# Rotating the late products over eight PSUM banks, splitting the last weight blocks into passes of 192 and 128 columns, and taking GpSimd out of the final norm

## The chip, the cores and the metric

The kernel runs on one core of one Trainium2 chip. The metric is the device time of one execution in microseconds (us), as a median over runs. Before the change it is 1042.79 us over three runs (1041.4 to 1043.75).

A core has five engines that run beside each other, each through its own instructions in order: PE (TensorE, matrix products into PSUM, with its weight loads shown apart as PEld), DVE (VectorE), ACT (ScalarE), POOL (GpSimd) and SP (SyncE, which here issues every DMA). PSUM has eight banks of 512 fp32 columns.

## The reference, cut to what matters

One decoder layer on 1024 prompt tokens and 64 sample tokens, 1088 columns in all, with a model width of 1024. The late part, which the change touches, is this:

```python
y_a = (o_a.astype(h.dtype) * jax.nn.silu(z_a)) @ w_up_gla
...
y_b = (o_b.astype(h.dtype) * jax.nn.silu(z_b)) @ w_up_gdn
merged = jax.nn.sigmoid(gate_a) * y_a + jax.nn.sigmoid(gate_b) * y_b
h = h + merged @ w_out
h = h + jax.nn.sigmoid(h @ w_ple_gate) * (p @ w_ple)
...
y = rms_norm(h, final_norm_w)
```

Ahead of it stand the input norm, the product with `w_in` (4,000-odd columns of projections) and two linear-attention recurrences; the change leaves them as they are.

## The kernel before, in words

Everything is kept transposed: the 128 partitions hold channels, the columns hold tokens. A width of 1024 is thus eight row blocks (m = 0 to 7) of 128 channels. The 1088 columns are cut into three chunks c, `CH = [(0, 384), (384, 384), (768, 320)]`.

**Products.** An fp32 product is made as three products of rounded halves: `w_split` (L169) cuts a 128x1024 weight block into a high half on ACT (`wh`, L173) and a low half on DVE (`wl`, L174), both float32r, and the operands are cut in the same way. `prod` (L290) then runs, for each of k = 8 row blocks, high by high, high by low and low by high, 24 matmuls into one PSUM bank (6 where k is 2). After every sixth matmul but the last it lets a list of side tasks advance by one tick (`sd.tick`); a side task is a generator that yields how many ticks it wants to wait.

**PSUM.** Two pools share the eight banks: `mp` has 3 banks (tile function `mps`, L145), `rp` has 5 (`rps`, L142). In the first two thirds of the program the 5 belong to the recurrences. In the late part every large product takes a bank of `mp`, and only the column sums of the final norm take one of `rp`.

**The late part (L1240 to L1430).** It has four stages: two branches (`py`, L1274, into M), the output product (`ho`, L1323, into H = residual + product), and the embedding stage with the final norm (L1383 to L1430). In the embedding stage, for a row block m and a chunk c, PE makes the gate product `eg` from Hh and Hl (24 matmuls) and the embedding product `ep` from ph and pl (6 matmuls). Then: ACT takes the tanh of `eg` into `et` (L1344); DVE computes (et + 1) * ep (L1420) and adds half of it to H (L1421); ACT squares H into `es` (L1425); DVE adds that to the running sum `acc` of the chunk (L1426); ACT scales H by the final norm's weight (L1428). Chunks 0 and 1 go together through m = 0 to 7; then chunk 2 goes through m = 0 to 7 with the eight weight blocks loaded and split a second time.

**The final norm of chunks 0 and 1** is a side task (`final`, L1349): a matmul with a matrix of ones sums `acc` over the partitions (`ssy`, L1354), then `normed` (L1358) takes Ln and Exp on ACT to get the reciprocal root `rsy` (L1367, L1368; these need another activation table than tanh, so there is a table load on either side), then eight products of H with `rsy` per chunk give `y` (L1379, and L1377 for the last one, which takes in the weight). Those for row blocks 2 and 5 are on POOL, the others on DVE. Each pair of row blocks leaves with one DMA (L1381).

**The end.** For m = 7 of chunk 2 the `ep` product goes first, ACT halves it (L1401), and after the `eg` product the chunk is cut into two halves of 160 columns. For each half: tanh, three DVE steps (L1407, L1410, L1411), a matmul of the squares with ones on top of the sums of the rows before (L1404, L1412), Ln, Exp, eight products (POOL takes rows 2 and 5), and DMAs of 2 + 2 + 4 row blocks for the first half, 4 + 4 for the second.

The order on each engine is set by the framework's scheduler from the program text, with a few fixed pairs (`after`). The weight pools hold three split blocks (`wh`, `wl`, 3 buffers each), so three of them can be kept at once.

Of the kernel before, what the change touches and what calls it, by code (L numbers as in the profile page):

```python
# [17 lines left out]
P = 128  # L18
# [4 lines left out]
EPS = 1e-6  # L23
NBLK = 34
NWARM = 4
SK = 2
UW, HW = 1116, 544
ORDER = ("h7 h3 g0 g2 h1 g1 k0 q0 a2 g3 h4 q1 k1 v0 a1 h5 q2 a0 "
# [75 lines left out]
def tile_hybrid_step(ctx: ExitStack, tc: tile.TileContext, xT, pT, wmain, wv0, wv1, wup, wout, wpg, wpl, wgate,  # L104
# [16 lines left out]
    def unit(name, dt=F32):  # L121
        return up.tile([P, UW], dt, tag="u", name=name)
# [13 lines left out]
    def wide(name):  # L136
        return up.tile([P, 384], F32, tag="wide", name=name, bufs=4)
# [44 lines left out]
    def w_next():  # L182
        if not wready:
            w_split()
        r = wready.pop(0)
        return r
# [115 lines left out]
    def xprod(ps, c, ws, hh, ll, lo_last=False):  # L302
        prod(ps, CH[c][1], ws, 0, lambda k: hh[c][:, k], lambda k: ll[c][:, k], 8, lo_last=lo_last)
# [944 lines left out]
    w_load()  # L1248
    w_load()


    M = [None] * 8

    def branch(br, og, first, after=None):
        for m in range(8):
            spilled = f"{'gh'[br]}{m}" in gscr
            while len(wready) < 2 - spilled:
                w_split()
            ws = None if spilled else w_next()
            us = w_next()  # L1260
            if first:
                M[m] = unit(f"M{m}") if m < 6 else lp.tile([P, UW], F32, tag="M", name=f"M{m}", bufs=2)
            for c, (o, w) in enumerate(CH):
                if spilled:
                    t = lp.tile([P, 384], F32, tag="gt", name=f"gt{br}{m}{c}", bufs=3)
                    load(t[:, :w], gscr[f"{'gh'[br]}{m}"][:, o:o + w])
                else:
                    pg = mps(f"pg{br}{m}{c}")
# [5 lines left out]
                py = mps(f"py{br}{m}{c}")  # L1274
# [39 lines left out]
    for m in range(8):  # L1314
        xres.append(unit(f"xres{m}"))
        load(xres[m][:, :T], xT[m])
        if m > 1:
            xres[m - 2] = None
        ws = w_next()
        w_split()  # L1320
        H[m] = unit(f"H{m}")
        for c, (o, w) in enumerate(CH):
            ps = mps(f"ho{m}{c}")  # L1323
            xprod(ps, c, ws, Mh, Ml)
            V.scalar_tensor_tensor(H[m][:, o:o + w], ps[:, :w], 0.5, xres[m][:, o:o + w], op0=ALU.mult, op1=ALU.add)  # L1325
            if m == 7:
                chunk(c)
        if m == 3:
            pr = []
            for k in range(2):  # L1330
                t = unit(f"pr{k}")
                load(t[:, :T], pT[k])
                pr.append(t)
            ph, pl, pchunk = split_pairs(pr, "p")
        if 3 < m < 7:
            pchunk(m - 4)
# [12 lines left out]
    def final(parts):  # L1349
        yield 0  # L1350
        pss = []
        for c, r, ac in parts:
            pss.append(rps(f"ssy{c}")[:, r])
            mm(pss[-1], ones, ac, start=True, stop=True)  # L1354
            yield 5
        yield from normed(parts, pss)

    def normed(parts, pss):  # L1358
        nonlocal exp
        acts = nc.scalar.preload_act_table_set("natural_log_exp_and_others").ins  # L1360
        after(acts, tanh)
        fw = pc[:, V_FW + 7:V_FW + 8]
        rss = []
        for n, (c, r, *_) in enumerate(parts):
            w = r.stop - r.start
            rs = wide(f"rsy{c}{r.start}")[:, :w]
            after(A.activation(rs, pss[n], AF.Ln, bias=eps_c, scale=1.0 / 1024).ins, exp if n else acts)  # L1367
            exp = A.activation(rs, rs, AF.Exp, scale=-0.5).ins  # L1368
            rss.append(rs)
        for n, (c, r, *_) in enumerate(parts):  # L1370
            w, o, rs = r.stop - r.start, CH[c][0] + r.start, rss[n]
            for m0, k in ((0, 2), (2, 2), (4, 2), (6, 2)) if w > 200 else ((0, 2), (2, 2), (4, 4)) if n == 0 else ((0, 4), (4, 4)):
                yt = unit(f"y{c}{n}{m0}")[:, :k * w].rearrange("p (m w) -> p m w", w=w)
                for j in range(m0, m0 + k):
                    e = H[j][:, o:o + w]
                    if j == 7:
                        V.scalar_tensor_tensor(yt[:, j - m0], e, fw, rs, op0=ALU.mult, op1=ALU.mult)  # L1377
                    else:
                        (G if j in (2, 5) else V).tensor_tensor(yt[:, j - m0], e, rs, op=ALU.mult)  # L1379
                yield 6  # L1380
                load(yT[m0:m0 + k, :, o:o + w].rearrange("m p w -> p m w"), yt)  # L1381

    for cs in ((0, 1), (2,)):  # L1383
        acc = {c: lp.tile([P, 384], F32, tag="acc", name=f"acc{c}", bufs=3) for c in cs}
        for m in range(8):
            ws = w_next()
            w_split()
            fw = pc[:, V_FW + m:V_FW + m + 1]
            for c in cs:
                o, w = CH[c]  # L1390
                hi, lo = (lambda k: ph[k][:, o:o + w]), (lambda k: pl[k][:, o:o + w])
                d = H[m][:, o:o + w]
                t, s = wide(f"et{m}{c}")[:, :w], wide(f"es{m}{c}")[:, :w]
                pg, pp = mps(f"eg{m}{c}"), mps(f"ep{m}{c}")
                if m == 7 and c == 2:

                    n = w // 2
                    prod(pp, w, wps[m // 4], 2 * (m % 4), hi, lo, 2)
                    hs = [slice(i * n, i * n + n) for i in range(2)]
                    pss = [rps(f"ssy{c}{i}")[:, :n] for i in range(2)]  # L1400
                    A.mul(s, pp[:, :w], 0.5)  # L1401
                    xprod(pg, c, ws, Hh, Hl)
                    for i, r in enumerate(hs):
                        mm(pss[i], ones, acc[c][:, r], start=True, stop=False)  # L1404
                    for i, r in enumerate(hs):
                        act_tanh(t[:, r], pg[:, r])
                        e = V.scalar_tensor_tensor(t[:, r], t[:, r], 1.0, s[:, r], op0=ALU.add, op1=ALU.mult).ins  # L1407
                        if i:
                            after(e, sq)
                        V.tensor_tensor(d[:, r], d[:, r], t[:, r], op=ALU.add)  # L1410
                        sq = V.tensor_tensor(s[:, r], d[:, r], d[:, r], op=ALU.mult).ins  # L1411
                        mm(pss[i], ones, s[:, r], start=False, stop=True)  # L1412
                    sd.until(lambda: not sd.tasks)
                    sd.spawn(normed([(c, r) for r in hs], pss))
                    sd.until(lambda: not sd.tasks)
                    continue
                xprod(pg, c, ws, Hh, Hl)
                prod(pp, w, wps[m // 4], 2 * (m % 4), hi, lo, 2)
                act_tanh(t, pg[:, :w])
                V.scalar_tensor_tensor(t, t, 1.0, pp[:, :w], op0=ALU.add, op1=ALU.mult)  # L1420
                V.scalar_tensor_tensor(d, t, 0.5, d, op0=ALU.mult, op1=ALU.add)  # L1421
                if m == 0:
                    A.activation(acc[c][:, :w], d, AF.Square)
                else:
                    A.activation(s, d, AF.Square)  # L1425
                    V.tensor_tensor(acc[c][:, :w], acc[c][:, :w], s, op=ALU.add)  # L1426
                if m < 7:
                    A.mul(d, d, fw)  # L1428
        if len(cs) == 2:
            sd.spawn(final([(c, slice(0, CH[c][1]), acc[c][:, :CH[c][1]]) for c in cs]))  # L1430


def _layout(i):
# [70 lines left out]
```

## Time and profile before

| | |
|---|---|
| median of three runs | 1042.79 us (1041.4 to 1043.75) |
| the profiled execution, its time | 1044.29 us |
| its span (first to last instruction on the core) | 1042.5 us |
| instructions in the profile | 17654 |
| granted TensorE clock, mean over the span | 0.986 |

The profiled execution's own time is 1.8 us above its span and 1.5 us above the median. The profile page gives busy time per engine, the span in 40 slices, the chain of work that ended last, and groups of instructions. In a row of the timeline the first number is the start in us from the span's start, the second the duration in us, and a bracket at the end is the idle time of the engine just before, with what ended it. A matmul's duration is longer than the step to the next one, because matmuls are pipelined; what a stream of them costs is read from the starts.

### The profile page before, as it was taken

How to read it: one execution, taken by the hardware profiler on the slowest of the kernel's cores; microseconds unless marked ns; L12 is line 12 of the kernel's file. 1: busy time of each engine (PE TensorE's matmuls, PEld its weight loads, DVE VectorE, ACT ScalarE, POOL GpSimd, SP SyncE). 2: the span in 40 equal slices, each digit the busy share in tenths (PEclk: the TensorE clock that was granted, in tenths of full speed). 3: DMA queues.
4: the chain of work that ended last, by engine and by line, in shares of the span. 5: the costliest groups of instructions: out<-in, count | busy, mean ns of one | idle time of the engine just before them, and what ended most of it. 6: DMA issues, size and time to landing. Idle time of an engine off the chain costs nothing.

```text
span 1042.5 us, 17654 instructions
## 1 busy us (share of the span) xinstructions
PE 1016.5 (98%) x7032; PEld 973.3 (93%) x7032; DVE 624.8 (60%) x1382; ACT 391.2 (38%) x934; POOL 71.3 (7%) x80
## 2 busy tenths in 40 slices
PE   7999999999899999999999999999999999999995
PEld 5889999999799998999899999999999999999995
DVE  6872824435767577776886567546378423554457
ACT  5552533324612633462345223323133202444353
POOL 4420010001100000100000000000000000000002
PEclk8989999999999999999999999999999999999998
DMA  8020012222122211231331222002455432221124
GB/s 314 1 70 33 22 36 90 95 87 53 54 67 75 77 57 51 56 96 58 96 87 43 74 86 85 21 24 82 138 154 152 147 126 105 62 81 50 52 81 172
DMA packets 67154, 86.34 MB, mean 83 GB/s; under 512 B 26812, under 2 KB 51312, under 8 KB 67072
## 3 DMA queue, kind: packets, MB, share of 16 engines
q1 hardware_dynamic: 67072, 85.22, 26.1%
q8 instruction: 55, 0.90, 0.4%
q14 instruction: 27, 0.22, 0.1%
HBM read 66.99 MB, written 18.21 MB: 82 GB/s over the span
## 4 chain that ended last, share of the span: by engine, by line
PE 85%; DVE 9%; issue 2%; ACT 2%; DMA 1%; POOL 0%; SPq 0%; DVEq 0%; ACTq 0%
PE ing L298 11%; PE py L298 9%; PE ho L298 9%; PE ingsh L298 8%; PE eg L298 8%; PE ingsg L298 8%; PE inza L298 4%; PE inzb L298 4%; PE ep L298 2%; PE inka L298 2%; PE v L402 2%; PE v L403 2%; PE v L404 2%; PE inqa L298 1%; DVE sqx L238 1%
## 5 line engine op out<-in xcount | busy, mean ns | idle before, releaser
L174 DVE TENSOR_TENSOR wl<-wr,wh 128x1024 fp32r<-128x1024 f32 x62 | 75.8, 1223 | 96.9 <-ACT wh L173 96.2
L173 ACT CAST wh<-wr 128x1024 fp32r<-128x1024 f32 x64 | 67.1, 1049 | 173.8 <-PE ho L298 40.8
L298 PE MATMUL ing<-xh,wh 128*128 128x384 f32 (+1 forms) x288 | 97.4, 338 | 0.0
L298 PE MATMUL ing<-xl,wh 128*128 128x384 f32 (+1 forms) x288 | 94.6, 329 | 0.0
L298 PE MATMUL ing<-xh,wl 128*128 128x384 f32 (+1 forms) x288 | 94.5, 328 | 0.0
L298 PE MATMUL ingsh<-xh,wh 128*128 128x384 f32 (+1 forms) x192 | 65.6, 342 | 0.0
L298 PE MATMUL ingsg<-xh,wh 128*128 128x384 f32 (+1 forms) x192 | 65.4, 341 | 0.0
L298 PE MATMUL eg<-Hh,wh 128*128 128x384 f32 (+1 forms) x192 | 63.4, 330 | 1.8 <-DVE et L1420 1.5
L298 PE MATMUL ingsg<-xl,wh 128*128 128x384 f32 (+1 forms) x192 | 63.0, 328 | 0.0
L298 PE MATMUL ingsh<-xl,wh 128*128 128x384 f32 (+1 forms) x192 | 62.9, 328 | 0.0
L298 PE MATMUL ingsh<-xh,wl 128*128 128x384 f32 (+1 forms) x192 | 62.9, 328 | 0.0
L298 PE MATMUL ingsg<-xh,wl 128*128 128x384 f32 (+1 forms) x192 | 62.9, 327 | 0.0
L298 PE MATMUL ho<-Mh,wl 128*128 128x384 f32 (+1 forms) x192 | 62.6, 326 | 0.0
L298 PE MATMUL eg<-Hh,wl 128*128 128x384 f32 (+1 forms) x192 | 62.6, 326 | 0.0
L298 PE MATMUL ho<-Ml,wh 128*128 128x384 f32 (+1 forms) x192 | 62.6, 326 | 0.0
L298 PE MATMUL ho<-Mh,wh 128*128 128x384 f32 (+1 forms) x192 | 62.6, 326 | 0.0
L298 PE MATMUL eg<-Hl,wh 128*128 128x384 f32 (+1 forms) x192 | 62.5, 326 | 0.0
L298 PEld LDWEIGHTS ing<-xh,wh 128*128 128x128 f32 x288 | 54.1, 188 | 2.1 <-issue 1.3
L298 PEld LDWEIGHTS ing<-xl,wh 128*128 128x128 f32 x288 | 54.2, 188 | 0.2 <-issue 0.2
L298 PEld LDWEIGHTS ing<-xh,wl 128*128 128x128 f32 x288 | 54.1, 188 | 0.2 <-issue 0.2
L781 DVE SCALAR_TENSOR_TENSOR D<-R,cw,D 128x1112 f32<-128x1112 f32 x36 | 49.4, 1373 | 1.9 <-ACT D L779 1.5
L1325 DVE SCALAR_TENSOR_TENSOR H<-ho,xres 128x384 f32<-128x384 f32 (+1 forms) x24 | 12.9, 536 | 57.0 <-PE ho L298 57.0
(420 smaller groups left out, 2813.9 us busy)
## 6 DMA issues: line engine op xcount, KB each, us to landing
wr<-in_wmain SPq DMA_DIRECT2D x40, 512.0 KB, 3.5
wr<-in_wpg SPq DMA_DIRECT2D x16, 512.0 KB, 3.5
xres<-in_xT SPq DMA_DIRECT2D x8, 544.0 KB, 4.5
wr<-in_wup SPq DMA_DIRECT2D x16, 256.0 KB, 2.9
wr<-in_wout SPq DMA_DIRECT2D x8, 512.0 KB, 3.6
xr<-in_xT SPq DMA_DIRECT2D x8, 384.0 KB, 8.4
gscrh<-gsh SPq DMA_DIRECT2D x16, 192.0 KB, 1.8
gscrg<-gsg SPq DMA_DIRECT2D x16, 192.0 KB, 1.8
```

The costliest lines, as they stand in the source:

```text
L173: a = A.copy(wh, wr).ins
L174: b = (eng or V).tensor_tensor(wl, wr, wh.bitcast(F32), op=ALU.subtract).ins
L238: V.tensor_tensor(xac[c], xac[c], sq, op=ALU.add)
L298: mm(ps[:, :w], l_, r_, start=i == 0, stop=i == len(seq) - 1)
L402: mm(ps[:, :n], h_, a_, start=k == 0, stop=False)
L403: mm(ps[:, :n], l_, a_, start=False, stop=False)
L404: mm(ps[:, :n], h_, b_, start=False, stop=k == 7)
L781: V.scalar_tensor_tensor(D[:, :n], R[:, i:n + i], cw[:, 4 * ci + i:4 * ci + i + 1], D[:, :n], op0=ALU.mult, op1=ALU.add)
L1325: V.scalar_tensor_tensor(H[m][:, o:o + w], ps[:, :w], 0.5, xres[m][:, o:o + w], op0=ALU.mult, op1=ALU.add)
```

## The change

It does three things.

1. `pps` deals the late products out over both pools in a fixed pattern of eight (3 from `mp`, 5 from `rp`), so that a bank comes round again after eight products instead of three. It replaces `mps` in the branches, the output product and the embedding stage, and `rps` for the sums of the final norm.
2. In the embedding stage, chunk 2 goes through m = 0 to 4 as before with 320 columns (`NLAST = 5`). Then m = 5, 6, 7 are run for columns 0 to 191 of the chunk, with their three split weight blocks kept; then the same three for columns 192 to 319. The norm of the first 192 columns is a side task that runs during the second pass; only that of the last 128 columns comes after the last product. The second pass's DMAs are 4 + 3 + 1 row blocks.
3. All eight products per chunk in `normed` are on DVE; POOL has none.

The diff, cut to its core (the three other places where `mps` becomes `pps` are left out):

```diff
+    npp = 0
+
+    def pps(name):
+        nonlocal npp
+        npp += 1
+        return (mps if npp % 8 in (0, 3, 6) else rps)(name)
...
-    def normed(parts, pss):
+    def normed(parts, pss, waits=6, sizes=(2, 2, 2, 2)):
...
-                        (G if j in (2, 5) else V).tensor_tensor(yt[:, j - m0], e, rs, op=ALU.mult)
-                yield 6
+                        V.tensor_tensor(yt[:, j - m0], e, rs, op=ALU.mult)
+                yield waits
                 load(yT[m0:m0 + k, :, o:o + w].rearrange("m p w -> p m w"), yt)
+                m0 += k
...
+    def embed(m, c, r, ws):
...
+        pg, pp = pps(f"eg{m}{c}"), pps(f"ep{m}{c}")
+
+        def gate():
+            prod(pg, w, ws, 0, lambda k: Hh[c][:, k, r], lambda k: Hl[c][:, k, r], 8)
+
+        if m == 7 and c == 2:
+
+            prod(pp, w, wps[1], 6, hi, lo, 2)
+            A.mul(s, pp[:, :w], 0.5)
+            gate()
+            ss = pps(f"ssy{c}{r.start}")[:, :w]
+            mm(ss, ones, ac, start=True, stop=False)
+            act_tanh(t, pg[:, :w])
+            V.scalar_tensor_tensor(t, t, 1.0, s, op0=ALU.add, op1=ALU.mult)
+            V.tensor_tensor(d, d, t, op=ALU.add)
+            V.tensor_tensor(s, d, d, op=ALU.mult)
+            return ss, s
+        gate()
+        prod(pp, w, wps[m // 4], 2 * (m % 4), hi, lo, 2)
+        act_tanh(t, pg[:, :w])
...
+    for m in range(NLAST):
+        ws = w_next()
+        w_split()
+        embed(m, 2, whole[2], ws)
+
+    def ending(r, ss, waits, sizes):
+        yield waits
+        mm(ss[0], ones, ss[1], start=False, stop=True)
+        yield from normed([(2, r)], [ss[0]], waits, sizes)
+
+    last = []
+    parts = slice(0, 192), slice(192, CH[2][1])
+    for m in range(NLAST, 8):
+        last.append(w_next())
+        w_split()
+        ss = embed(m, 2, parts[0], last[-1])
+    sd.until(lambda: not sd.tasks)
+    sd.spawn(ending(parts[0], ss, 2, (2, 2, 2, 2)))
+    for m in range(NLAST, 8):
+        ss = embed(m, 2, parts[1], last[m - NLAST])
+    sd.until(lambda: not sd.tasks)
+    sd.spawn(ending(parts[1], ss, 0, (4, 3, 1)))
+    sd.until(lambda: not sd.tasks)
```

How the order moves, at three places. First DVE in chunk 2, around row blocks 5 and 6: `y` are the products of the norm of chunks 0 and 1, `et`, `H` and `acc` the steps of the embedding stage. Before:

```order
L1420 SCALAR_TENSOR_TENSOR et_10171<-et_10171,ep_10174 128x320
L1379 TENSOR_TENSOR y_10325<-H_8819,rsy_10137 128x384
L1421 SCALAR_TENSOR_TENSOR H_8910<-et_10171,H_8910 128x320
L1379 TENSOR_TENSOR y_10329<-H_9001,rsy_10137 128x384
L1377 SCALAR_TENSOR_TENSOR y_10329<-H_9092,pc,rsy_10137 128x384
L1426 TENSOR_TENSOR acc_9923<-acc_9923,es_10172 128x320
L1420 SCALAR_TENSOR_TENSOR et_10215<-et_10215,ep_10218 128x320
```

And now:

```order
L1388 TENSOR_TENSOR y_10317<-H_8910,rsy_10137 128x384
L1388 TENSOR_TENSOR y_10321<-H_9001,rsy_10137 128x384
L1386 SCALAR_TENSOR_TENSOR y_10321<-H_9092,pc,rsy_10137 128x384
L1421 SCALAR_TENSOR_TENSOR et_10171<-et_10171,ep_10174 128x192
L1422 SCALAR_TENSOR_TENSOR H_8910<-et_10171,H_8910 128x192
L1427 TENSOR_TENSOR acc_9233<-acc_9233,es_10172 128x192
L1421 SCALAR_TENSOR_TENSOR et_10215<-et_10215,ep_10218 128x192
L1422 SCALAR_TENSOR_TENSOR H_9001<-et_10215,H_9001 128x192
L1427 TENSOR_TENSOR acc_9233<-acc_9233,es_10216 128x192
```

Before, the steps of row block 5 (`et_10171`) stood among the last products of the norm; now all sixteen products of chunks 0 and 1 stand ahead of them, and the two additions to `acc` follow behind.

Second PE at the end of chunk 2's products: `eg` is a gate product, `ssy` a column sum with the matrix of ones. Before:

```order
L298 MATMUL eg_10261<-Hl_9208,wh 128x320
L298 MATMUL eg_10261<-Hh_9207,wl 128x320
L1404 MATMUL ssy_10269<-acc_9923,ones 128x160
L1404 MATMUL ssy_10270<-acc_9923,ones 128x160
L1412 MATMUL ssy_10269<-es_10260,ones 128x160
L1412 MATMUL ssy_10270<-es_10260,ones 128x160
```

And now, where the first pass (`eg_10261`) ends and the second (`eg_10327`) begins:

```order
L299 MATMUL eg_10261<-Hl_9208,wh 128x192
L299 MATMUL eg_10261<-Hh_9207,wl 128x192
L1412 MATMUL ssy_10294<-acc_9233,ones 128x192
L299 MATMUL eg_10327<-Hh_9207,wh 128x128
L299 MATMUL eg_10327<-Hl_9208,wh 128x128
```

The sum of `acc` stood behind the last product of all; now one stands between the two passes, ahead of the 90 products of the second.

Third ACT at the end: `et` is a tanh, `rsy` Ln and Exp. Before:

```order
L1401 ACTIVATE es_10260<-ep_10262 128x320
L1428 ACTIVATE H_9001<-H_9001,pc 128x320
L1344 ACTIVATE et_10259<-eg_10261 128x160 x2
L1360 ACT_TABLE_LOAD
L1367 ACTIVATE rsy_10334<-ssy_10269,eps_t 128x160
```

And now, in the second pass:

```order
L1352 ACTIVATE et_10325<-eg_10327 128x128
L1368 ACT_TABLE_LOAD
L1426 ACTIVATE es_10326<-H_8910 128x128
L1429 ACTIVATE H_8910<-H_8910,pc 128x128
L1375 ACTIVATE rsy_10377<-ssy_10294,eps_t 128x192
L1376 ACTIVATE rsy_10377<-rsy_10377 128x192
L1352 ACT_TABLE_LOAD
L1352 ACTIVATE et_10365<-eg_10367 128x128
```

The norm of the first 192 columns, with a table load on either side, stands between the tanh of row block 5 and that of row block 6 of the second pass.

More of the change, by code (lines that the diff above doesn't have):

```diff
@@ L1371, in normed @@
             w, o, rs = r.stop - r.start, CH[c][0] + r.start, rss[n]
-            for m0, k in ((0, 2), (2, 2), (4, 2), (6, 2)) if w > 200 else ((0, 2), (2, 2), (4, 4)) if n == 0 else ((0, 4), (4, 4)):
-                yt = unit(f"y{c}{n}{m0}")[:, :k * w].rearrange("p (m w) -> p m w", w=w)
+            m0 = 0
+            for k in sizes:
+                yt = unit(f"y{c}{r.start}{m0}")[:, :k * w].rearrange("p (m w) -> p m w", w=w)
                 for j in range(m0, m0 + k):
@@ L1378, in normed @@
                     else:
-                        (G if j in (2, 5) else V).tensor_tensor(yt[:, j - m0], e, rs, op=ALU.mult)
-                yield 6
+                        V.tensor_tensor(yt[:, j - m0], e, rs, op=ALU.mult)
+                yield waits
                 load(yT[m0:m0 + k, :, o:o + w].rearrange("m p w -> p m w"), yt)
[L1383 to L1430, printed above, removed]
@@ new lines, in tile_hybrid_step @@
+    whole = [slice(0, w) for _, w in CH]
+    for m in range(8):
+        ws = w_next()
+        w_split()
+        for c in (0, 1):
+            embed(m, c, whole[c], ws)
+    sd.spawn(final([(c, whole[c], acc[c][:, whole[c]]) for c in (0, 1)]))
+    for m in range(NLAST):
+        ws = w_next()
+        w_split()
[4 more added lines that the diff above has]
+        yield from normed([(2, r)], [ss[0]], waits, sizes)
```

24 lines of the change are left out of this document (20 added, 4 removed).

## The prediction

> **What bounds the kernel now.** I read the chain that ended last first, then the windows of the last two stages, then the timeline of each engine there.
>
> ```profile
> PE 85%; DVE 9%; issue 2%; ACT 2%; DMA 1%; POOL 0%; SPq 0%; DVEq 0%; ACTq 0%
> ```
>
> ```profile
> 1015.30:1030.80 15.50, 13.74 (x92) 13.15 (x91) 13.89 (x22) 7.22 (x14) 4.72 (x4) 1.00 0.55 205
> 1030.80:1042.50 11.70, 1.87 (x10) 1.18 (x9) 6.20 (x18) 3.24 (x7) 2.34 (x4) 0.77 0.36 112
> ```
>
> The first row is the chain's shares by engine; in the window rows stand length, then busy time of PE, PEld, DVE, ACT and POOL, then the granted clock. PE bounds the program up to about 1031 us, and a serial tail of 11.7 us follows. Within the 15.5 us ahead of that tail PE misses about 1.8 us, and DVE is nearly as busy as PE (13.89 us).
>
> ```profile
> 1015.37 0.30 PE L298 MATMUL eg<-Hh,wh 128*128 128x320 f32 x1
> ...
> 1018.74 0.31 PE L298 MATMUL eg<-Hh,wl 128*128 128x320 f32 x1
> ...
> 1021.47 0.42 PE L298 MATMUL eg<-Hh,wh 128*128 128x320 f32 x1 [1.46 <-DVE et L1420]
> ...
> 1027.29 0.41 PE L298 MATMUL eg<-Hh,wh 128*128 128x320 f32 x1 [0.30 <-ACT et L1344]
> ...
> 1030.77 0.31 PE L298 MATMUL eg<-Hh,wl 128*128 128x320 f32 x1
> 1030.92 0.71 PE L1404 MATMUL ssy<-acc,ones 128*128 128x160 f32 x4
> ```
>
> These are PE's rows for m = 5, 6 and 7 of chunk 2. The first two rows are the first and last of 24 gate matmuls, so a matmul of 320 columns takes a step of 3.37 / 23 = 0.1465 us. The brackets are the two places where PE waits for a bank of the pool of three.
>
> **The bank rotation** takes these two waits away (1.46 + 0.30, some 2.3 us with the slow restarts). The rest of the late part has no such wait in the list of waits, so it gains nothing. Whether the 2.3 us reach the end depends on what PE meets next.
>
> **The narrow passes.** The 90 matmuls of m = 5, 6, 7 (three blocks of 30) become 90 of 192 columns and 90 of 128. No row of before shows a float32r matmul that narrow; these bound it:
>
> ```profile
> 85.91 0.28 PE L402 MATMUL v<-wvh,xh 128*128 128x264 f32 x1
> ...
> 86.27 0.29 PE L402 MATMUL v<-wvh,xh 128*128 128x264 f32 x1
> ```
>
> ```profile
> 285.94 0.19 PEld L298 LDWEIGHTS inza<-xl,wh 128*128 128x128 f32 x1
> 286.05 0.19 PEld L298 LDWEIGHTS inza<-xh,wl 128*128 128x128 f32 x1
> ```
>
> ```profile
> 145.91 0.30 PEld L513 LDWEIGHTS gds<-gd,K 128*128 128x128 f32 x2
> ...
> 146.58 0.30 PEld L516 LDWEIGHTS gds<-gd,K 128*128 128x128 f32 x2
> ```
>
> ```profile
> L514 PE MATMUL gds<-gd,K x2: 252/252/253, 146.2 to 146.3; 128*128 128x4 f32 x2
> ```
>
> From below: 264 columns take 0.12 (three steps in 0.36), 320 take 0.1465, so by the columns alone 192 would take 0.09 and 128 some 0.065. But each matmul loads its own 128x128 weights. Two float32r loads with nothing between them start 0.11 apart, and six loads of the `gds` sums (4 to 32 columns, so next to no streaming) go from 145.91 to 146.58, 0.1115 each. I take 0.1115 for both widths, as the nearest row: the load sets the step. From above, plain fp32: the four records at 1030.92 (two products of 160 columns) end after 0.71, the last lasting 0.30, so 0.136 a record and two records a product, which scaled by columns makes 0.326 at 192 and 0.217 at 128. Taken: the first pass 90 x 0.1115 = 10.0 us, the second as much, against 90 x 0.1465 = 13.2 before: +6.9 us of PE. That is the price of the shorter tail.
>
> **What PE meets next.** Between the passes stands the sum of `acc` (the order's second place), which needs the additions of m = 5 and 6. Those stand behind all sixteen products of the norm on DVE (the first place).
>
> ```profile
> 1015.27 3.62 DVE L1379 TENSOR_TENSOR y<-H,rsy 128x384 f32<-128x384 f32 x4 [0.84 <-ACT rsy L1368]
> 1018.81 1.21 DVE L174 TENSOR_TENSOR wl<-wr,wh 128x1024 fp32r<-128x1024 f32 x1
> ...
> 1026.33 0.55 DVE L1379 TENSOR_TENSOR y<-H,rsy 128x384 f32<-128x384 f32 x1
> 1026.80 0.61 DVE L1377 SCALAR_TENSOR_TENSOR y<-H,pc,rsy 128x384 f32<-128x384 f32 x1
> 1027.33 0.48 DVE L1426 TENSOR_TENSOR acc<-acc,es 128x320 f32<-128x320 f32 x1
> 1027.73 0.47 DVE L1420 SCALAR_TENSOR_TENSOR et<-et,ep 128x320 f32<-128x320 f32 x1
> 1028.24 0.49 DVE L1421 SCALAR_TENSOR_TENSOR H<-et,H 128x320 f32<-128x320 f32 x1
> 1029.27 0.49 DVE L1426 TENSOR_TENSOR acc<-acc,es 128x320 f32<-128x320 f32 x1 [0.54 <-ACT es L1425]
> ```
>
> ```profile
> 1015.31 2.69 POOL L1379 TENSOR_TENSOR y<-H,rsy 128x384 f32<-128x384 f32 x2 [312.35 <-ACT rsy L1368]
> ```
>
> ```profile
> 1028.77 0.47 ACT L1425 ACTIVATE es<-H 128x320 f32<-128x320 f32 x1 [1.08 <-DVE H L1421]
> 1029.14 0.42 ACT L1401 ACTIVATE es<-ep 128x320 f32<-128x320 f32 x1
> ```
>
> While POOL runs its products, four on DVE take 3.62 us, 0.9 each; with POOL idle one takes a step of 0.47 (1026.33 to 1026.80). So taking POOL out is worth it: fourteen products at 0.47, two of the L1377 kind at 0.53, the weight split at 1.2 and the three steps of m = 4 at 0.40 are 10.0 us, from 1015.27 to 1025.3. That is sooner than before, but only then does DVE turn to m = 5. From there a step of 320 columns takes 0.51 to the next (1027.73 to 1028.24), 0.53 to the square, 0.50 to the addition, 0.49 for it; 128 columns less take off 0.14 each (at 0.07 per 64 columns, from 0.47 at 384 to 0.40 at 320). So m = 5 from `et` to its square 0.76, two ACT steps 0.70, the tanh of m = 6 0.37, `et` to its square 0.76, the addition 0.71: 3.3 us, done at 1028.6. ACT takes the tanh of m = 6 only after the square of m = 5, so this chain can't be shortened by PE. PE, free of bank waits, ends the first pass at 1015.37 + 10.0 = 1025.4, and waits **3.2 us** in front of the whole second pass. The wait removed comes back here, and the first pass's own price is hidden in it.
>
> **What the wait does to the clock.**
>
> ```profile
> 262.39:265.80 3.41, 0.92 (x9) 0.77 (x8) 3.41 (x7) 3.32 (x15) 0.00 (x0) 1.00 0.00 0
> 265.80:269.22 3.42, 3.42 (x25) 2.87 (x24) 1.10 (x3) 3.34 (x10) 0.00 (x0) 0.50 0.40 129
> ```
>
> ```profile
> 265.06 0.63 PE L646 MATMUL kr<-K,QK 128*128 128x128 f32 x4 [2.49 <-DVE QK L640]
> ```
>
> ```profile
> 23.46:26.80 3.34, 3.34 (x14) 3.34 (x13) 0.98 (x2) 3.11 (x8) 0.00 (x0) 0.50 0.43 177
> ```
>
> ```profile
> L253 PEld LDWEIGHTS ssr<-ones,sqx x6: 190/333/333, 23.1 to 24.2; 128*128 128x128 f32 x6
> ```
>
> After PE waited 2.49 us the clock was granted at 0.50 for the next 3.41 us; after the wait of 1.46 us above it stayed at 1.00. 3.2 us is the longer, so I count one stretch at half clock. There a load takes 0.22 (five steps from 23.1 to 24.2), so 3.41 us hold 15.5 matmuls instead of 30.6, a loss of 15.1 x 0.1115 = 1.7 us. The Trainium skill ("TensorE: Matmul & The Clock Gate", section "HAM oscillation — how this bites in real kernels") has the rule that idle gaps between matmuls are to stay below some 3.4 us. By that rule this gap would do nothing and the sum be 1.7 us less; the trace disagrees, with a half clock after 2.49 us, and the trace decides.
>
> **The second pass.** The `acc` sum of 192 columns takes 0.33 (two records of 0.163), so the pass begins at 1028.95. With 89 x 0.1115 = 9.9, the second sum inside it (0.33) and 1.7 for the clock, its last gate matmul starts at 1040.9; before it was 1030.77, so +10.1 us. The first part's four DMAs go out on SP meanwhile, with nobody waiting for them. Its inputs are there in time: the norm of the first part on ACT and DVE, with two more table loads, ends near 1037, beside PE.
>
> **The tail.**
>
> ```profile
> 1031.12 0.50 ACT L1344 ACTIVATE et<-eg 128x160 f32<-128x160 f32 x2 [1.10 <-PE eg L298]
> 1031.63 1.28 ACT L1360 ACT_TABLE_LOAD   x1
> ```
>
> ```profile
> 1034.05 2.57 DVE L1379 TENSOR_TENSOR y<-H,rsy 128x160 f32<-128x160 f32 x5 [0.53 <-ACT rsy L1368]
> ...
> 1036.84 1.25 DVE L1379 TENSOR_TENSOR y<-H,rsy 128x160 f32<-128x160 f32 x5
> 1038.02 0.37 DVE L1377 SCALAR_TENSOR_TENSOR y<-H,pc,rsy 128x160 f32<-128x160 f32 x1
> ```
>
> ```profile
> 1034.97 3.86 SPq L1381 DMA_DIRECT2D out_yT<-y  x5
> ```
>
> ```profile
> SPq L1500 <- DMA out_yT<-y: 2.5, 1, 2.5
> ```
>
> ```profile
> out_yT<-y SPq DMA_DIRECT2D x2, 160.0 KB, 1.9
> ```
>
> Before, 1030.77 to the first product 3.28 us, to the last issue 7.7, to the end 11.73. After: 32 columns less in eight serial steps, 2.95 us to the first product; seven products at 0.20 (1.18 / 5 at 160 columns, less 0.033) and the last at 0.34, against sixteen at up to 0.51 beside POOL: 4.7 us. The pieces leave 0.47 apart on SP, the last (one row block, 64 KB) at 5.0. I give it 1.6 to land, below the 1.9 of 160 KB, and the 1.1 that follows the landing now: 7.7 us, a gain of 4.0.
>
> **The sum:** 1042.5 + 10.1 - 4.0 = 1048.6 for the span. The profiled span lies 0.3 below the median of the runs (1042.79), so 1048.9 us, 0.6% slower. A measurement here tells about 0.2% (2.1 us) from no change.
>
> **The rivals.**
> - *Faster: the array's own pace.* The narrow matmuls take 0.09 and 0.065, and DVE is through with m = 6 before the first pass ends. Then the last gate matmul starts at 1015.37 + 8.1 + 0.66 + 5.8 = 1029.9, and 1029.9 + 7.7 + 0.3 = **1037.9**. It would turn to a gain from a last gate matmul ahead of 1034.8. For it: the line through 264 and 320 columns. Against: load spacing of 0.11, and the order on DVE. Chance 0.05.
> - *The fast pace, but the wait stands.* The second pass begins at 1028.95 and is then bound by ACT and DVE: its first gate ends at 1030.8, tanh and a table load (1.28) to 1032.3, two narrow steps, Ln and Exp to 1033.65, eight products of 192 columns to 1035.9, `et`, `H`, square, scaling and halving to 1037.25, the tanh to 1037.5, which is 0.6 after where a last gate matmul would stand. 1036.9 + 7.7 + 0.3 = **1044.9**. The Trainium skill (same page, section "Back-to-back issue gap") gives some 81 ns per matmul for a stream of loads and matmuls of 128 columns; by that estimate the pass takes 7.3 us, and no run here shows it for float32r. Chance 0.10.
> - *The load sets the step, but nothing waits at the sum.* Last gate matmul at 1015.37 + 10.0 + 0.66 + 9.9 = 1036.0; **1044.0**, within the noise. Against: sixteen products ahead of m = 5. Chance 0.07.
> - *Narrow float32r at the price of plain fp32.* 0.326 and 0.217: 1015.37 + 29.3 + 0.66 + 19.3 + 7.7 + 0.3 = **1072.7**. Only the upper bound speaks for it. Chance 0.06.
>
> **How the numbers follow.** My forecast has the remaining 0.72, about 0.5 of it with the half clock and 0.2 without (1047.2). Loads of 0.108 or matmuls of 0.12 move the second pass by -0.3 or +0.8, a second stretch at half clock adds 1.7, the DVE chain and the tail 0.5 each: 1046.5 to 1051. With the rival at 1044.9 the range is 1044.8 to 1051.0; outside are the first, third and last rival. Faster by over 0.2% is the first rival, 0.05; within 0.2% the third and half of the second, 0.12; slower the rest, 0.83.
>
> **What would show it.** Right: a wait of about 3 us before the `acc` sum between the passes, released by DVE's `acc` (L1427); steps of 0.11 in both passes; a granted clock of 0.50 soon after; last gate matmul to end 7.7 us. Wrong: steps near 0.065 in the second pass, or no wait at that sum (then the DVE rows are mis-sized), or steps above 0.2.

## The result, and the profile after the change

| | before | after |
|---|---|---|
| median of five runs each | 1043.75 us (1041.4 to 1043.93) | 1058.02 us (1054.5 to 1059.28) |
| ratio, 95% interval | | 1.0138 (1.0117 to 1.0158) |
| span of the profiled execution | 1042.5 us | 1056.2 us |

The change makes the kernel 1.4% slower. The profiled span grows by 13.7 us: chunk 2 starts 1.0 us sooner than in the profiled execution of before (the part ahead of it differs by some us between executions), it takes 18.2 us longer up to the last gate matmul, and the tail is 3.5 us shorter.

These are the windows of the changed kernel: first pass, wait, second pass, tail. Columns are length, busy time of PE, PEld, DVE, ACT and POOL, granted clock, DMA share, GB/s.

```profile
1014.25:1024.58 10.33, 10.33 (x93) 10.16 (x91) 10.29 (x21) 4.82 (x9) 0.00 (x0) 1.00 0.65 239
1024.58:1027.70 3.12, 0.00 (x1) 0.00 (x0) 1.80 (x6) 1.80 (x6) 0.00 (x0) 0.80 0.61 226
1027.70:1048.34 20.64, 20.63 (x95) 20.63 (x95) 5.12 (x17) 5.98 (x14) 0.00 (x0) 0.50 0.12 39
1048.34:1056.24 7.90, 1.44 (x5) 0.85 (x4) 2.64 (x11) 2.24 (x4) 0.00 (x0) 0.50 0.22 66
```

About the same number of matmuls (a window also counts those that only reach into it) take 10.33 us in the first pass and 20.64 in the second. PE counts as busy for all of both; only the clock column tells them apart. PE's rows in the timeline show the step and the wait:

```profile
1014.39 0.25 PE L299 MATMUL eg<-Hh,wh 128*128 128x192 f32 x1
...
1024.30 0.28 PE L299 MATMUL eg<-Hh,wl 128*128 128x192 f32 x1
1027.71 1.01 PE L1412 MATMUL ssy<-acc,ones 128*128 128x192 f32 x2 [3.13 <-DVE acc L1427]
1028.26 0.56 PE L299 MATMUL eg<-Hh,wh 128*128 128x128 f32 x1
1028.62 0.41 PE L299 MATMUL eg<-Hl,wh 128*128 128x128 f32 x1
...
1030.97 0.41 PE L299 MATMUL eg<-Hh,wh 128*128 128x128 f32 x1
...
1048.03 0.41 PE L299 MATMUL eg<-Hh,wl 128*128 128x128 f32 x1
```

The first pass takes 9.91 / 89 = 0.1113 us a step. Then PE waits 3.13 us for `acc`. In the second pass eleven steps take 2.35 us, 0.2136 each. DVE's rows show what the sum waited for:

```profile
1014.29 1.97 DVE L1388 TENSOR_TENSOR y<-H,rsy 128x384 f32<-128x384 f32 x4 [0.84 <-ACT rsy L1376]
...
1023.73 0.61 DVE L1386 SCALAR_TENSOR_TENSOR y<-H,pc,rsy 128x384 f32<-128x384 f32 x1
1024.26 0.34 DVE L1421 SCALAR_TENSOR_TENSOR et<-et,ep 128x192 f32<-128x192 f32 x1
...
1027.30 0.36 DVE L1427 TENSOR_TENSOR acc<-acc,es 128x192 f32<-128x192 f32 x1 [0.43 <-ACT es L1426]
```

Four products take 1.97 us where they took 3.62 beside POOL. All sixteen still stand ahead of m = 5, whose `et` starts at 1024.26, 9.97 us after the first product; `acc` of m = 6 follows at 1027.30. Last, windows of 3.41 us, the grid on which the clock changes:

```profile
1023.04:1026.45 3.41, 1.54 (x14) 1.37 (x13) 2.60 (x7) 1.04 (x3) 0.00 (x0) 1.00 1.04 387
1026.45:1029.86 3.41, 2.15 (x9) 2.15 (x10) 1.82 (x6) 1.26 (x4) 0.00 (x0) 0.50 0.00 0
1029.86:1033.28 3.42, 3.42 (x18) 3.42 (x18) 0.00 (x0) 0.00 (x0) 0.00 (x0) 0.50 0.00 0
...
1043.52:1046.93 3.41, 3.41 (x18) 3.41 (x18) 0.00 (x0) 0.18 (x2) 0.00 (x0) 0.50 0.00 0
```

The stretch in which PE was busy for 1.54 us is followed by half clock. It never comes back: 0.50 holds from 1026.45 to the end at 1056.2, through stretches in which PE is busy for all of the time.

### The profile page after: what moved, and what is told of

Same layout as the page of the kernel before. It is cut to its first block, busy times and chain, and to the rows that moved or that the text cites. A ratio compares the mean times of both kernels' runs of the same rounds, so it can differ in the third digit from the quotient of the medians.

```text
span 1056.2 us, 17822 instructions
## 1 busy us (share of the span) xinstructions
PE 1030.6 (98%) x7122; PEld 987.4 (93%) x7122; DVE 624.5 (59%) x1396; ACT 395.7 (37%) x943; POOL 64.5 (6%) x72
## 4 chain that ended last, share of the span: by engine, by line
PE 81%; DVE 10%; issue 6%; ACT 2%; DMA 1%; POOLq 0%; SPq 0%; POOL 0%; DVEq 0%
PE ing L299 11%; PE py L299 9%; PE eg L299 9%; PE ho L299 9%; PE ingsh L299 8%; PE ingsg L299 8%; PE inza L299 4%; PE ep L299 2%; PE inka L299 2%; PE inzb L299 2%; PE v L403 1%; PE v L404 1%; PE v L405 1%; PE inqa L299 1%; DVE sqx L239 1%
## 5 line engine op out<-in xcount | busy, mean ns | idle before, releaser
L299 PE MATMUL eg<-Hh,wh 128*128 128x384 f32 (+3 forms) x216 | 72.5, 336 | 0.0
L299 PE MATMUL eg<-Hh,wl 128*128 128x384 f32 (+3 forms) x216 | 71.7, 332 | 0.0
L299 PE MATMUL eg<-Hl,wh 128*128 128x384 f32 (+3 forms) x216 | 71.7, 332 | 0.0
```

Source lines behind the costliest of these rows:

```text
L299: mm(ps[:, :w], l_, r_, start=i == 0, stop=i == len(seq) - 1)
```

## The experiments

Before and after the change differ by 14 us where some 6 were forecast, and the second pass, at 0.50 from its start to its end, is where most of that lies. Theory, in the expectations also called sticky: the wait at the sum lowers the clock, and the narrow matmuls behind it don't bring it back. Rivals: the narrow matmuls alone lower it; or a drop here lasts some 30 us whatever follows. All kernels of one batch shared their runs of before; each ratio is against those.

### The sum moved behind the products (no wait)

```diff
-            mm(ss, ones, ac, start=True, stop=False)
...
-            return ss, s
+            return ss, s, ac
...
     def ending(r, ss, waits, sizes):
         yield waits
+        mm(ss[0], ones, ss[2], start=True, stop=False)
         mm(ss[0], ones, ss[1], start=False, stop=True)
```

> The sum of acc (ones x acc) of each part stands with the sum of squares behind it instead of ahead of the second pass; nothing else changes. Sticky theory: the wait of 3.1 us between the passes lowers the clock, and matmuls of 128 columns, whose streaming fills under half of their step (0.053 of 0.111 us), keep it from being granted again. Without the wait the clock stays at 1.00 through the second pass, its steps are 0.11 us, the last gate matmul starts 20.3 us after the first of row block 5, and the time is within 0.3% of before (about 1043 to 1045 us). Rival, narrow matmuls alone: the clock falls to 0.50 within two stretches of 3.4 us of the second pass though nothing waits, its steps are 0.213 us from there, and the time is 1050 us or more.

Measured: 1045.29 us, ratio 1.0020 (1.0009 to 1.0032). Windows of the first pass, the second pass and the tail:

```profile
1015.25:1025.28 10.03, 10.03 (x93) 10.03 (x91) 10.03 (x21) 4.66 (x8) 0.00 (x0) 1.00 0.65 240
1025.28:1036.70 11.42, 10.95 (x97) 10.65 (x95) 6.89 (x23) 7.57 (x18) 0.00 (x0) 1.00 0.39 136
1036.70:1044.33 7.63, 0.91 (x6) 0.53 (x5) 2.64 (x11) 2.24 (x4) 0.00 (x0) 0.65 0.24 71
```

Without the wait at the sum the same 128-column matmuls run at 1.00 to the last one, and the ratio falls from 1.0138 to 1.0020. So 128 columns alone don't lower the clock. A short wait is left inside the pass, for the squares of the first 192 columns, and the clock stays at 1.00 behind it:

```profile
1030.28 0.59 PE L1445 MATMUL ssy<-es,ones 128*128 128x192 f32 x2 [0.47 <-DVE es L1415]
```

A whole stretch of the second pass holds 34 records where the changed kernel had 18:

```profile
1025.32:1028.73 3.41, 3.41 (x34) 3.41 (x32) 1.92 (x6) 1.98 (x6) 0.00 (x0) 1.00 0.60 221
```

### 128 columns first, and 160 and 160

```diff
-    parts = slice(0, 192), slice(192, CH[2][1])
+    parts = slice(0, 128), slice(128, CH[2][1])
```

(and 160 in the other kernel)

> The passes change places: 128 columns first, then 192; the wait between them stays. Sticky theory: the first pass runs its 90 matmuls of 128 columns at a clock of 1.00 in steps of 0.11; the wait of some 2 to 3 us lowers the clock, and the second pass of 192 columns (0.080 of 0.111 us streaming) gets it back after one or two stretches of 3.4 us: about 1046 to 1049 us. Narrow matmuls alone: the clock falls in the first pass, before any wait. Long hold (a drop at this place lasts some 30 us whatever follows): half clock through the second pass too, 1056 us or more.

> Both passes have 160 columns. Streaming then fills 0.067 of a step of 0.111 us, 60%. Sticky theory: the wait between the passes lowers the clock as before; if a little over half is enough the second pass gets it back after one or two stretches of 3.4 us and the time is 1046 to 1049 us; if the boundary lies above 60% it stays at 0.50 to the end, 1056 to 1059 us. Long hold: 0.50 to the end. Narrow matmuls alone: no fall in the first pass either way, since 192 columns did not have one and 160 lie near.

Measured with 128 first: 1047.95 us, ratio 1.0051 (1.0034 to 1.0067). The wait and the windows around it:

```profile
1025.57 0.38 PE L1412 MATMUL ssy<-acc,ones 128*128 128x128 f32 x1 [1.63 <-DVE acc L1427]
```

```profile
1023.04:1026.45 3.41, 1.78 (x17) 1.64 (x15) 2.49 (x8) 1.13 (x5) 0.00 (x0) 1.00 0.91 334
1026.45:1029.86 3.41, 3.41 (x19) 3.41 (x17) 0.45 (x2) 0.00 (x0) 0.00 (x0) 0.50 0.00 0
1029.86:1033.28 3.42, 3.42 (x32) 3.42 (x32) 1.07 (x3) 2.80 (x6) 0.00 (x0) 1.00 0.00 0
```

One stretch at half clock, then full clock again under 192 columns. With 160 and 160: 1056.97 us, ratio 1.0139 (1.0124 to 1.0154), and 0.50 to the end behind this wait:

```profile
1027.35 0.63 PE L1412 MATMUL ssy<-acc,ones 128*128 128x160 f32 x1 [2.21 <-DVE acc L1427]
```

So a drop here need not last 30 us, and the long-hold rival falls. But the two kernels differ in the wait too (1.63 and 2.21 us), so the width wasn't yet shown to decide.

### Wide matmuls behind the same wait

```diff
         ss = embed(m, 2, parts[0], last[-1])
+    xprod(pps("wide"), 0, last[-1], Hh, Hl)
```

> The changed kernel with one more product of 24 matmuls of 384 columns, unused, between the sum of acc and the second pass; the wait of about 3 us ahead of the sum stays. Theory (the wait lowers the clock, and matmuls of 128 columns keep it low where wide ones give it back): the clock falls to 0.50 after the wait, comes back to 1.00 within one or two stretches of 3.41 us inside the wide product, which takes about 5.5 us, and stays there; the second pass then runs at 0.111 a step, 10.3 us with its sum, and the tail takes 7.7 us: about 1052 us, 6 us less than the changed kernel although it does more work. Rival (a wait of 3 us lowers the clock for some 30 us whatever follows): the wide product takes 7.7 us at 0.32 a matmul, the second pass 19.8 us as in the changed kernel, 1066 us.

Measured: 1054.26 us, ratio 1.0100 (1.0082 to 1.0118). The windows from the wait on:

```profile
1027.61:1031.02 3.41, 2.68 (x8) 2.68 (x9) 1.43 (x4) 1.18 (x4) 0.00 (x0) 0.50 0.00 0
1031.02:1034.43 3.41, 3.41 (x12) 3.41 (x12) 0.00 (x0) 0.00 (x0) 0.00 (x0) 0.50 0.00 0
1034.43:1037.84 3.41, 3.41 (x29) 3.41 (x27) 0.00 (x0) 0.00 (x0) 0.00 (x0) 1.00 0.00 0
1037.84:1041.26 3.42, 3.42 (x33) 3.42 (x31) 0.87 (x3) 2.60 (x6) 0.00 (x0) 1.00 0.02 5
```

After one stretch filled with 384 columns the clock is back. The second pass then takes 10.2 us from its first row to its last, and the kernel is faster than the changed one with 24 matmuls more (ratio 1.0100 against 1.0138):

```profile
1035.74 0.22 PE L299 MATMUL eg<-Hh,wh 128*128 128x128 f32 x1
...
1045.95 0.28 PE L299 MATMUL eg<-Hh,wl 128*128 128x128 f32 x1
```

### 192 or 160 columns behind the same wait

```diff
         ss = embed(m, 2, parts[0], last[-1])
+    for _ in range(2):
+        prod(pps("wide"), 192, last[-1], 0, lambda k: Hh[0][:, k, :192], lambda k: Hl[0][:, k, :192], 8)
```

> The changed kernel with two more products of 24 matmuls each, 192 columns, unused, between the sum of acc and the second pass; the wait of about 3.1 us stays as it is in the changed kernel. Theory (the width of what follows the wait decides, and 192 columns suffice): 0.50 for one or two stretches inside the added matmuls (0.2132 a step), then 1.00, and the second pass at 0.111: 8.6 us added, 10.3 us for the pass, 1057. Rival (the length of the wait decides: after 1.6 us 192 columns got the clock back, after 3.1 us they don't): 0.50 to the end, 10.2 us added and 19.8 us for the pass, 1068.

> The same with 160 columns in the two added products. Theory (the width decides, and 160 columns don't suffice): 0.50 from the wait to the end, the added matmuls and the second pass at 0.2132 a step, 1068. Rival (160 columns give the clock back too, and the passes of 160 and 160 stayed low for another reason): 1.00 after one or two stretches, 1057.

Measured: 1054.52 us with 192, ratio 1.0101 (1.0071 to 1.0130); 1067.74 us with 160, ratio 1.0227 (1.0198 to 1.0257); two runs each. First the windows with 192, then those with 160:

```profile
1024.37:1027.78 3.41, 2.71 (x12) 2.71 (x12) 1.43 (x4) 1.15 (x4) 0.00 (x0) 0.50 0.00 0
1027.78:1031.20 3.42, 3.42 (x18) 3.42 (x17) 0.00 (x0) 0.00 (x0) 0.00 (x0) 0.50 0.00 0
1031.20:1034.61 3.41, 3.41 (x32) 3.41 (x32) 0.00 (x0) 0.00 (x0) 0.00 (x0) 1.00 0.00 0
```

```profile
1030.30:1033.72 3.42, 3.42 (x18) 3.42 (x18) 0.00 (x0) 0.00 (x0) 0.00 (x0) 0.50 0.00 0
...
1037.13:1040.54 3.41, 3.41 (x18) 3.41 (x18) 0.00 (x0) 0.00 (x0) 0.00 (x0) 0.50 0.02 5
```

The wait is 3.14 and 3.13 us, the stretch that decides has 18 records and PE busy throughout in both, and only the width differs. 192 columns bring the clock back and 160 don't. What differs is the number of columns that go through in a stretch: it holds 3.41 / 0.2133 = 16 matmuls (18 records with those that reach over its edges), so 3070 or 2560 columns.

### Narrow matmuls without the wait

If columns per stretch are what counts, narrow enough matmuls must lose the full clock without any wait. A first try put passes of 240 and 80, and of 216 and 104, into the kernel with the late sum:

```diff
-    parts = slice(0, 192), slice(192, CH[2][1])
+    parts = slice(0, 240), slice(240, CH[2][1])
```

> The kernel with the late sum (no wait at the sum of acc), passes of 240 and 80 columns instead of 192 and 128. New theory, read from the runs so far: the clock of a stretch of 3.41 us follows from how many columns PE ran through in the stretch before, whatever the waits; all stretches with some 2700 columns or less were followed by 0.50 (also 160 columns at half clock, 16 x 160 = 2560), all with some 3050 or more by 1.00 (192 at half clock, 16 x 192 = 3070; 128 at full clock, 30.6 x 128 = 3920). 80 columns at full clock are 30.6 x 80 = 2450: the clock falls to 0.50 in the middle of the second pass though PE waits for nothing there, after 3.4 to 6.8 us, and stays: the pass takes some 14.5 us instead of 10.3, about 1049 us. Rival (only a wait takes the full clock away; narrow matmuls merely keep it from coming back): 1.00 to the end of the pass, 1045 us.

> The same with passes of 216 and 104 columns. New theory (columns per stretch, bound between 2700 and 3050): 30.6 x 104 = 3180 columns, the clock stays at 1.00 through the second pass, 1045 us. Rival (it is the share of a matmul's step that its columns fill, and it has to be about half, as with 128 columns): 104 columns fill 0.42 of their step, the clock falls in the pass as with 80 columns, 1049 us.

Measured: 1050.46 us (ratio 1.0084, 1.0061 to 1.0107) and 1050.6 us (1.0065, 0.9996 to 1.0135). This decided nothing: with shorter second passes the wait for the squares of the first part, 0.47 us above, grew to 0.98 and 0.75 us, and the drop came right behind it. The three runs with 104 columns were 1043.46, 1050.6 and 1051.45 us, with a granted clock of 0.992, 0.983 and 0.982 over the span, so the same program kept or lost the clock from run to run. The second try puts three unused products of 80 or of 104 columns between the passes of 192 and 128 of the kernel with the late sum, where nothing is waited for:

```diff
         ss = embed(m, 2, parts[0], last[-1])
+    for _ in range(3):
+        prod(pps("narrow"), 80, last[-1], 0, lambda k: Hh[0][:, k, :80], lambda k: Hl[0][:, k, :80], 8)
```

> The kernel with the late sum, passes of 192 and 128, with three unused products of 24 matmuls of 80 columns each between the passes, where PE waits for nothing (the passes of 80 and of 104 columns still had a wait of 0.98 and 0.75 us for the squares inside, so they didn't tell). Theory (columns per stretch of 3.41 us: at or below 2700 the next is at 0.50, at or above 3050 at 1.00): 30.6 x 80 = 2450, the clock falls to 0.50 inside the added matmuls after the first stretch that they fill, and the second pass of 128 doesn't get it back: some 20 us more than the late sum's 1045, 1065 us. Rival (only a wait takes the full clock away): 1.00 to the end of the second pass, 8 us more, 1053 us.

> The same with 104 columns in the added products. Theory: 30.6 x 104 = 3180 columns a stretch, the clock stays at 1.00 until the end of the second pass, 8 us more than the late sum's 1045, 1053 us. Rival (the columns must fill about half of a step, or the bound lies higher): the clock falls inside the added matmuls as with 80 columns, 1065 us.

Measured: 1065.86 us with 80, ratio 1.0221 (1.0183 to 1.0259); 1051.71 us with 104, ratio 1.0085 (1.0053 to 1.0117); two runs each. First the windows with 80, then those with 104:

```profile
1024.04:1027.45 3.41, 3.41 (x33) 3.41 (x33) 2.13 (x7) 1.55 (x5) 0.00 (x0) 1.00 0.73 268
1027.45:1030.86 3.41, 3.41 (x18) 3.41 (x18) 1.28 (x4) 0.74 (x3) 0.00 (x0) 0.50 0.00 0
1030.86:1034.28 3.42, 3.42 (x18) 3.42 (x18) 0.00 (x0) 0.00 (x0) 0.00 (x0) 0.50 0.02 5
```

```profile
1026.81:1030.23 3.42, 3.42 (x34) 3.42 (x32) 1.66 (x5) 1.26 (x4) 0.00 (x0) 1.00 0.00 0
1030.23:1033.64 3.41, 3.41 (x33) 3.41 (x33) 0.00 (x0) 0.00 (x0) 0.00 (x0) 1.00 0.02 5
```

With 80 columns a stretch in which PE is busy for all 3.41 us is followed by 0.50; with 104 the clock stays. The wait is one way to get few columns into a stretch; width is another.

### Without the passes, and its two parts alone

The rotation and the norm without POOL, put into the kernel before; then each alone. The one-line part is:

```diff
-                        (G if j in (2, 5) else V).tensor_tensor(yt[:, j - m0], e, rs, op=ALU.mult)
+                        V.tensor_tensor(yt[:, j - m0], e, rs, op=ALU.mult)
```

> The kernel before with the eight-bank rotation and the norm's products all on DVE, without the passes. All theories: PE's two bank waits (1.46 and 0.30 us, 2.3 with the restarts) go and nothing takes their place, since no sum of acc stands inside the products; DVE alone makes the sixteen products of the tail in 3.8 to 4.1 us against 4.3: 2.3 to 2.8 us faster than before, 0.997 to 0.998. A rival for this part alone: DVE's sixteen products of chunks 0 and 1 then hold up the last tanh or the last sum, and the gain stays under 1 us.

> The kernel before with the late products and the norm's sums dealt over all eight banks, GpSimd still in the norm, no passes. The late kernel without passes was 4.3 us faster than before, and its span was made of 2.4 us less in chunk 2, 0.9 us less in the tail and some 1 us that lies in the early part and differs from one execution to the next. Theory (each part gives its own share): the two bank waits (1.46 and 0.30 us) go, PE gets to the sum of acc about 2.3 us sooner, near 1028.5, but with GpSimd beside it DVE finishes acc of m = 6 near 1029.8 as before, so a wait of 1 us or more opens at that sum, and only about 1 us is gained: 1042. Rival (the rotation is the whole gain in chunk 2): no such wait, some 2.4 us gained, 1040.6. Second rival (the gain is GpSimd's alone): 1043, no change.

> The kernel before with all products of the norm on DVE, the three-bank pool kept, no passes. Theory (each part gives its own share): a product takes 0.49 instead of 0.9 us on DVE, so the step of m = 4 that releases PE's bank comes about 1 us sooner and the bank wait falls from 1.46 us to some 0.5; the tail is 0.9 us shorter; together about 2 us gained, 1041. Rival (the rotation is the whole gain in chunk 2): the bank wait stays near 1.5 us and only the tail's 0.9 us is gained, 1042. Second rival (GpSimd is the whole gain): no bank wait is left and the time is that of the kernel without passes, 1039.

| | us | ratio, 95% interval |
|---|---|---|
| both, no passes | 1038.74 | 0.9962 (0.9947 to 0.9977) |
| rotation only | 1041.45 | 0.9984 (0.9974 to 0.9993) |
| norm without POOL only | 1038.95 | 0.9961 (0.9947 to 0.9974) |

Windows of chunk 2 and of the tail: before, both parts, the rotation alone, the norm alone.

```profile
992.13:1030.80 38.67, 36.91 (x245) 35.79 (x245) 26.67 (x41) 19.96 (x36) 4.72 (x4) 1.00 0.41 137
```

```profile
990.59:1026.99 36.40, 36.40 (x245) 35.87 (x245) 25.19 (x45) 19.95 (x36) 0.00 (x0) 1.00 0.40 134
1026.99:1037.70 10.71, 1.76 (x10) 1.06 (x8) 5.83 (x22) 3.24 (x7) 0.00 (x0) 0.78 0.49 159
```

```profile
989.88:1026.28 36.40, 36.40 (x245) 35.76 (x244) 25.91 (x40) 18.74 (x34) 6.77 (x4) 1.00 0.41 139
1026.28:1038.78 12.50, 2.02 (x10) 1.16 (x8) 6.69 (x19) 4.35 (x10) 2.35 (x4) 0.72 0.38 122
```

```profile
990.61:1027.12 36.51, 36.51 (x245) 35.90 (x245) 25.23 (x45) 19.96 (x36) 0.00 (x0) 1.00 0.38 134
1027.12:1037.79 10.67, 1.76 (x10) 1.06 (x8) 5.83 (x22) 3.24 (x7) 0.00 (x0) 0.77 0.49 160
```

Either part takes both bank waits away (38.67 to 36.40 or 36.51 us). The rotation alone pays some of that back: PE reaches the sum of `acc` sooner than DVE and waits 0.86 us there, and the stretch behind chunk 2 is 12.50 us.

```profile
1027.30 0.81 PE L1411 MATMUL ssy<-acc,ones 128*128 128x160 f32 x4 [0.86 <-DVE acc L1433]
```

POOL out does more than the theory gave it, as the second rival had it. DVE's rows, first of before and then with the norm alone on DVE, show the first product and the `et` that releases PE's bank:

```profile
1015.27 3.62 DVE L1379 TENSOR_TENSOR y<-H,rsy 128x384 f32<-128x384 f32 x4 [0.84 <-ACT rsy L1368]
...
1020.94 0.47 DVE L1420 SCALAR_TENSOR_TENSOR et<-et,ep 128x320 f32<-128x320 f32 x1
```

```profile
1013.74 1.96 DVE L1379 TENSOR_TENSOR y<-H,rsy 128x384 f32<-128x384 f32 x4 [0.84 <-ACT rsy L1368]
...
1017.70 0.47 DVE L1420 SCALAR_TENSOR_TENSOR et<-et,ep 128x320 f32<-128x320 f32 x1
```

That `et` ends 4.4 us after the first product begins instead of 6.1, so no wait is left for the rotation to remove. Both together measure as that part alone; no version here is faster than these two.

### One block in two passes, with the late sum

```diff
-NLAST = 5
+NLAST = 7
```

> The changed kernel with only the last weight block in passes of 192 and 128 columns (instead of the last three) and with the sum of acc moved behind the products, next to the sum of the squares. Theory (the passes cost 0.0765 us for each matmul of 320 columns that is split, and the wait is gone): 30 x 0.0765 = 2.3 us more on PE than the kernel without passes, the tail between its 10.8 and the 7.75 us of the kernel with the late sum, since the second pass of 3.35 us is too short to cover the first part's norm: about 8.7; 1038.7 + 2.3 - 2.1 = 1039, no half clock in the passes. Rival (the passes pay once nothing waits): below 1037. Second rival (the first part's norm on DVE stands in front of the second part's steps and the tail is no shorter than 10.8 us): 1041 or more.

Measured: 1042.17 us, ratio 0.9989 (0.9980 to 0.9999). Windows of chunk 2 and of the tail:

```profile
989.05:1027.71 38.66, 38.66 (x276) 38.13 (x275) 26.26 (x48) 20.47 (x38) 0.00 (x0) 1.00 0.38 137
1027.71:1038.99 11.28, 1.57 (x10) 1.19 (x9) 4.85 (x19) 4.20 (x7) 0.00 (x0) 0.77 0.37 116
```

Against the kernel without passes the pass costs 2.26 us (38.66 against 36.40; 2.3 expected), and the tail gets no shorter (11.28 against 10.71, where 8.7 was expected), which is the second rival's outcome. A pass of 3.3 us doesn't cover the first part's norm: on DVE its eight products start at 1031.62, 3.9 us after the pass has ended, and those of the last 128 columns stand behind them, at 1033.84. The passes pay neither for three blocks nor for one.

## Why the prediction was right or wrong

- **The step of the narrow matmuls** (0.1115 for 192 and 128, the loads setting it): right at full clock, 0.1113 in the first pass; the kernel with the late sum runs 34 records in 3.41 us with 128 columns, and the second pass behind the wide product takes 0.1147 a step, its sum included. At half clock a step is 0.2133, near the 0.22 that the prediction read off the loads. The array-pace rivals and the plain-fp32 one fall with it.
- **The wait at the sum** (3.2 us, released by DVE's `acc`, behind sixteen products): right, 3.13 us.
- **What the wait does to the clock: this step failed.** The prediction counted "one stretch at half clock", 1.7 us, and allowed for a second. The drop itself was right. But from the second pass's first gate matmul to the last, 1028.26 to 1048.03, 19.77 us pass, where the same pass takes 10.2 us behind the wide product: 9.6 us lost in place of 1.7, which is 7.9 us more, where the span missed by 7.6 in all. The row that it rested on, 0.50 for 3.41 us after a wait of 2.49, is about other matmuls behind the wait: plain fp32 ones, of which the prediction's own rows give 0.136 us for a record of 160 columns, nearly the 0.1465 of a float32r matmul of 320. What follows decides how long half clock lasts, and the prediction priced the drop without asking whether 128-column matmuls could end it.
- **The rule of idle gaps.** The Trainium skill ("TensorE: Matmul & The Clock Gate", section "HAM oscillation — how this bites in real kernels") has the rule that idle gaps stay below some 3.4 us, by which shorter ones would do nothing. The prediction sided with the trace, and the runs bear the prediction out: 0.50 follows waits of 3.13, 2.21 and 1.63 us. The Trainium skill (same page, section "What's actually happening") says that the clock comes back after one window of some 3.4 us of sustained activity. The runs agree for 192 and 384 columns, and disagree for 128 and 160, with PE busy throughout and 0.50 to the end.
- **The tail** (7.7 us from the last gate matmul): 8.2 (1048.03 to 1056.24), half a us more, all at half clock.
- **The bank waits** (they go, and come back as another wait): right for the changed kernel. Not seen: taking POOL out removes them by itself.
- **The rival without a wait** (1044.0): the late sum made it, at 1045.29. Even so the passes cost: by the windows above they take 10.03 + 11.42 = 21.45 us for what 90 steps of 0.1465 did in 13.2, and the tail is 3.1 us shorter than without passes (7.63 against 10.71), 5.2 us in all. The spans of the two profiled executions lie 6.6 us apart, 1044.3 and 1037.7; the other 1.4 lie ahead of chunk 2, which starts at 992.01 and 990.59, in the part that differs between executions.

By the prediction's own sum: -1.0 for the start of chunk 2, +0.3 up to the second pass, +7.8 in the second pass, +0.5 in the tail, 7.6 us above the 1048.6 forecast for the span.

## What to carry to other kernels

When a trace shows a wait ahead of narrow matmuls, price the clock for all of the narrow stretch, not for one window, and ask whether what follows is wide enough to end it; a PE that waits and a PE that spends its steps on weight loads had the same effect here. Before adding machinery for a wait, look at what the releasing engine is slowed by: here one line that took POOL's products to DVE removed the waits for which the bank rotation was made. A pass over fewer columns costs its load-bound steps in full, and pays only if the shorter tail is worth more.

## What the runs showed of the hardware

- In these runs the clock follows how many columns PE puts through in a stretch of 3.41 us, not how long PE is busy. Worked out from steps and widths, stretches with up to some 2800 columns were followed by 0.50 (12 x 192 ahead of the wait in the changed kernel, 16 x 160 at half clock, 3 x 192 and 28 x 80 without a wait), and those with 3070 or more by 1.00 (16 x 192 at half clock, 30.6 x 104 = 3180 and 30.6 x 128 = 3920 at full clock). The same estimate, from each matmul's start and width, can be made for every stretch of the sixteen traces in which PE ran float32r products and next to nothing else, 2683 of them: the 60 below 2950 columns were followed by 0.50, the 2616 above 3200 by 1.00, and the seven between went either way (8 x 384 = 3072, from 10.61 us on in the kernel with two added products of 192 columns, was followed by 0.50). So the bound lies near 3000; where it is exactly, and what the chip counts, these runs leave open.
- A load-bound float32r matmul takes 0.111 to 0.112 us at full clock and 0.2133 at half, whether it has 80 or 192 columns. At half clock a stretch of 3.41 us thus holds 16 of them, and products of 80, 128 and 160 columns kept themselves at 0.50.
- Four products of two SBUF tensors on DVE take 1.97 us alone and 3.62 beside the same kind of product on POOL. The Trainium skill ("SBUF — State Buffer", section "SBUF: two separate sides") says that the two engines share a pair of ports, and that the one which starts first holds it for its whole instruction. The rows agree in that DVE is slowed; who held the ports when, they don't show.
- With passes of 216 and 104 columns one program gave 1043.46 us in one run and 1051.45 in another. The wait of 0.75 us can fall within one stretch or across two, which would explain it; this isn't shown, since only one of these runs has a profile.
